# Gates of half the token groups made for all experts at once, the rest with joined high and low sums, and top-k paced

## Chip, cores and metric

The kernel runs on one core of one Trainium2 chip. The metric is the device time of one execution in microseconds (us), lower is better. A profile of one execution shows the core's engines: TensorE (PE; PEld is its weight load), VectorE (DVE), ScalarE (ACT), GpSimd (POOL) and SyncE (SP), and the DMA queues.

## What is computed

A first block (a gated recurrent mixer, then a PEER expert layer) and two attention blocks with feed-forward layers behind it, for 256 tokens of width 1024. The change is in the PEER layer alone:

```python
q = (t @ w_q).reshape(n_tok, PEER_HEADS, 2, PEER_HALF)          # 8 heads, two halves of 128
sc = jnp.einsum("thpk,hpnk->thpn", q, sub_keys)                 # 128 keys per half
s_top, i_top = lax.top_k(sc, PEER_TOPK)                         # 16 of 128, per token, head, half
cand = s_top[:, :, 0, :, None] + s_top[:, :, 1, None, :]
cand_idx = i_top[:, :, 0, :, None] * PEER_NKEYS + i_top[:, :, 1, None, :]
best, pos = lax.top_k(cand.reshape(n_tok, PEER_HEADS, 256), PEER_TOPK)
idx = jnp.take_along_axis(cand_idx.reshape(n_tok, PEER_HEADS, 256), pos, axis=-1)
g = jax.nn.softmax(best, axis=-1)
act = jax.nn.gelu(jnp.einsum("phkd,pd->phk", u_tab[idx], tb))   # 16384 experts of width 1024
out = jnp.einsum("phk,phkd->pd", g * act, v_tab[idx])
```

## The kernel before

The kernel gathers nothing. It computes the gelu products of all 16384 experts with all tokens and multiplies them by a gate that is zero where a token didn't choose an expert. The experts are 128 rows (the first index, `i`) of 128 (the second index, on the partitions).

- **q stage** (16 blocks): `weight(("q", c))`, 24 matmuls, the scores of the block before (`scores`), and x2t, the scaled input of the u stage.
- **u stage** (128 blocks, `u_block`): block i loads a 512 KB weight tile of expert row i, multiplies it with the tokens (24 matmuls of 256 columns, in three products of high and low parts: lines 209 to 211), and ScalarE writes the gelu to H, 256 columns for each row i. H lies in three pieces: rows 0 to 31, 32 to 63, 64 to 127.
- **v stage** (128 blocks): the pair of H rows is split to ph and pl (`gated`), and 12 matmuls of 512 columns (`add_k`, line 237) add it into four accumulators.

Each f32 weight tile `raw` is split into whi (ScalarE, line 188) and wlo (DVE, line 189), three tiles ahead of its use; the PE's second product of a block needs wlo.

Beside this main work runs a background generator, which `pump(n)` steps on after each block. Where a step's instructions come to stand on their engines is decided by a scheduler when the kernel is built, from what they depend on. The generators are:

- `topk()`, 90 steps at 1.6 per u block (PK) from block 0 on in the program, though the scheduler lets its first searches start in the q stage: 32 steps of the search among 128 keys (`topk1`: MAX8, FIND_INDEX8, MATCH_REPLACE8, MAX8, FIND_INDEX8 on the DVE), and then per half of the tokens the sums of candidates, the second search, the lookup of indices (products on POOL, TENSOR_REDUCE on the DVE), softmax and three transposes. It yields i1T, i2T (the two indices of each chosen expert) and gT (gate, high and low part in f16).
- `gates(0)` beside u blocks 64 to 127 and `gates(1)` beside v blocks 0 to 63. Both go over the tokens in 32 groups of 8 (TB). For a group, the DVE builds eb (one-hot of the second index, 128 x 1024 f16), ea (one-hot of the first index, 64 rows of it) and ahl (ea times gT, high and low), the PE sums them with 16 matmuls of 64 columns (line 838, 8 tokens, high and low), and the DVE multiplies the sums into H (line 844): rows 0 to 63 in `gates(0)`, rows 64 to 127 in `gates(1)`.

```python
for t in range(TB):
    g, j = t // TI, t % TI
    for q in range(2):
        pe.matmul(gps[:, t, :], eb[:, g, :, j], ahl[:, g, :, q, j], start=q == 0, stop=q == 1)
```

The gate sums and the u products share four rotating PSUM banks (`bank`); the v accumulators have four of their own.

Of the kernel before, what the change touches and what calls it, by code (L numbers as in the profile page):

```python
# [29 lines left out]
TB = 8  # L30
# [3 lines left out]
PK = 1.6  # L34
PG = 1.6
# [24 lines left out]
def kernel(  # L60
# [588 lines left out]
    with pctx:  # L649
# [54 lines left out]
        def topk():  # L704
            for tt in range(2):
                for c in range(16):
                    topk1(tt, c, c % 2)
                    yield
# [14 lines left out]
            for tt in range(2):  # L723
# [26 lines left out]
                for hh in range(8):  # L750
# [36 lines left out]

        for c in range(17):
# [22 lines left out]
        background(topk())  # L811
        Hs, H23 = [], []
# [7 lines left out]
        def gates(s):  # L820
            for t0 in range(0, T, TB):
                eb = gp.tile([128, TG, 128, TI], F16, tag="eb", name=f"eb{s}_{t0}", bufs=2)
                dve.tensor_tensor(eb, spread(i2T, t0, 128), iE.unsqueeze(1).to_broadcast([128, TG, 128, TI]),
                                  op=OP.is_equal)
                ea = gp.tile([128, TG, 64, TI], F16, tag="ea", name=f"ea{s}_{t0}", bufs=1)
                dve.tensor_tensor(ea, spread(i1T, t0, 64),
                                  iE[:, s * 64:s * 64 + 64, :].unsqueeze(1).to_broadcast([128, TG, 64, TI]),
                                  op=OP.is_equal)
                yield
                ahl = gp.tile([128, TG, 64, 2, TI], F16, tag="ahl", name=f"ahl{s}_{t0}")  # L830
                dve.tensor_tensor(ahl, ea.unsqueeze(3).to_broadcast([128, TG, 64, 2, TI]),
                                  gT[:, t0 // TI:t0 // TI + TG].unsqueeze(2).to_broadcast([128, TG, 64, 2, TI]),
                                  op=OP.mult)
                gps = bank([128, TB, 64], f"g{s}_{t0}")
                for t in range(TB):
                    g, j = t // TI, t % TI
                    for q in range(2):
                        pe.matmul(gps[:, t, :], eb[:, g, :, j], ahl[:, g, :, q, j], start=q == 0, stop=q == 1)  # L838
                yield
                for h0, n in ((0, 32), (32, 32)) if s == 0 else ((0, 64),):  # L840
                    hv = Hs[2 * s + h0 // 32][:, 0:n * T] if s == 0 else H23[0]
                    hv = hv.rearrange("p (i t) -> p i t", t=T)[:, :, t0:t0 + TB]
                    gv = gps[:, :, h0:h0 + n].rearrange("p t i -> p i t")
# [643 lines left out]
```

## Time and profile before

| | us |
|---|---|
| median of 3 runs (lowest to highest) | 1728.07 (1724.71 to 1732.78) |
| the profiled execution | 1727.79 |
| its span, first to last instruction | 1726.0 |
| PE, DVE, ACT busy in it | 1680.5, 1207.7, 884.9 |
| u stage, first to last product | 266.7 to 674.1 |
| v stage, first to last product | 674.2 to 1061.5 |

A recorded matmul is longer than the distance to the next one, since matmuls are pipelined; so costs on the PE are read from the starts of neighbours, not from the recorded durations.

### The profile page before, as it was taken

Reading aid. Unit: us, or ns where it says so; the run is one execution under the profiler, and the core shown is the slowest. Engines: PE = TensorE matmul, PEld = TensorE weight load, DVE = VectorE, ACT = ScalarE, POOL = GpSimd, SP = SyncE. Lnnn points to the kernel's source line nnn. Section 1 sums busy time; section 2 is a strip of 40 time slices with the busy share of each in tenths; the row PEclk is TensorE's granted clock in tenths of the full one; section 3 lists DMA queues with packets and bytes.
Section 4 is the critical chain, followed back from the end, with each engine's and each line's share of the span. In section 5 each row is a group of like instructions: output and inputs, shape, how many; then the busy total and the mean of one; then the engine's idle time right before and its main releaser. Section 6 shows DMA issues by size and latency. Waiting matters only on the chain.

```text
span 1726.0 us, 30134 instructions
## 1 busy us (share of the span) xinstructions
PE 1680.5 (97%) x11917; PEld 1535.0 (89%) x11917; DVE 1207.7 (70%) x2174; ACT 884.9 (51%) x1446; POOL 127.4 (7%) x104
## 2 busy tenths in 40 slices
PE   8999999999999999999999999989999999999997
PEld 8998899899999999887888888877999889989997
DVE  7969699985477776878755555876766665567665
ACT  6686565454443344344444443665655455545552
POOL 2023010430000000000000001341000000000000
PEclk9999999999999999999999999999999999999999
DMA  7645546455544445456565555632755544347551
GB/s 243 194 161 165 201 147 221 151 182 181 182 154 153 157 152 170 159 159 195 171 219 187 191 192 183 224 112 78 239 191 188 184 154 141 116 138 222 184 184 49
DMA packets 90574, 296.63 MB, mean 172 GB/s; under 512 B 9201, under 2 KB 20545, under 8 KB 89665
## 3 DMA queue, kind: packets, MB, share of 16 engines
q1 hardware_dynamic: 89088, 293.66, 52.1%
q8 instruction: 93, 1.52, 0.4%
q10 hardware_dynamic: 1344, 1.05, 0.2%
q14 instruction: 49, 0.39, 0.1%
HBM read 289.39 MB, written 3.19 MB: 170 GB/s over the span
## 4 chain that ended last, share of the span: by engine, by line
PE 81%; DVE 8%; ACT 5%; DMA 3%; issue 2%; POOL 1%; POOLq 0%; SPq 0%; ACTq 0%; DVEq 0%
PE pv L237 21%; PE ff L237 6%; PE u L209 6%; PE u L210 6%; PE u L211 6%; PE g L838 4%; DVE wlo L189 3%; PE fg L209 2%; PE fg L211 2%; PE fg L210 2%; PE fu L209 2%; PE fu L211 2%; PE fu L210 2%; PE ul L1034 1%; PE wo L237 1%
## 5 line engine op out<-in xcount | busy, mean ns | idle before, releaser
L189 DVE TENSOR_TENSOR wlo<-raw,whi 128x1024 fp32r<-128x1024 f32 x383 | 471.9, 1233 | 207.8 <-ACT whi L188 204.1
L188 ACT ACTIVATE whi<-raw 128x1024 fp32r<-128x1024 f32 x383 | 404.7, 1057 | 257.3 <-PE pv L237 122.4
L189 DVE TENSOR_TENSOR W<-raw,W 128x1024 fp32r<-128x1024 f32 x150 | 186.0, 1243 | 119.9 <-ACT W L188 119.3
L210 PE MATMUL u<-xn2h,wlo 128*128 128x256 f32 x928 | 262.5, 283 | 5.9 <-DVE wlo L189 5.8
L209 PE MATMUL u<-xn2h,whi 128*128 128x256 f32 x928 | 264.1, 285 | 0.0
L211 PE MATMUL u<-xn2l,whi 128*128 128x256 f32 x928 | 261.5, 282 | 0.0
L188 ACT ACTIVATE W<-raw 128x1024 fp32r<-128x1024 f32 x150 | 158.6, 1061 | 167.0 <-PE pv L237 68.5
L210 PEld LDWEIGHTS u<-xn2h,wlo 128*128 128x128 f32 x928 | 175.0, 189 | 8.4 <-DVE wlo L189 8.3
L209 PEld LDWEIGHTS u<-xn2h,whi 128*128 128x128 f32 x928 | 175.4, 189 | 0.0
L211 PEld LDWEIGHTS u<-xn2l,whi 128*128 128x128 f32 x928 | 174.7, 188 | 0.0
L863 ACT ACTIVATE H<-u 128x256 f32<-128x256 f32 x128 | 49.1, 384 | 220.3 <-PE u L211 220.1
L237 PE MATMUL pv<-W,ph 128*128 128x512 f32 x416 | 116.2, 391 | 0.0
L237 PE MATMUL pv<-whi,pl 128*128 128x512 f32 x304 | 96.1, 395 | 0.0
L237 PE MATMUL pv<-wlo,ph 128*128 128x512 f32 x304 | 95.5, 394 | 0.0
L237 PE MATMUL pv<-whi,ph 128*128 128x512 f32 x304 | 95.1, 402 | 0.0
L844 DVE SCALAR_TENSOR_TENSOR H<-g,H 128x256 f32<-128x256 f32 (+1 forms) x96 | 46.2, 509 | 68.3 <-PE g L838 68.3
L237 PEld LDWEIGHTS pv<-W,ph 128*128 128x128 f32 x416 | 77.7, 188 | 16.2
L838 PE MATMUL g<-ahl,eb 128*128 128x64 f16 x1024 | 73.1, 238 | 0.0
L838 PEld LDWEIGHTS <-eb 128*128 128x128 f16 x1024 | 60.3, 114 | 12.2 <-issue 9.3
L237 PEld LDWEIGHTS pv<-wlo,ph 128*128 128x128 f32 x304 | 57.1, 188 | 13.5
L237 PEld LDWEIGHTS pv<-whi,pl 128*128 128x128 f32 x304 | 57.0, 189 | 13.3
L237 PEld LDWEIGHTS pv<-whi,ph 128*128 128x128 f32 x304 | 55.7, 190 | 10.9
(843 smaller groups left out, 4244.0 us busy)
## 6 DMA issues: line engine op xcount, KB each, us to landing
raw<-in_uT_dram SPq DMA_DIRECT2D x128, 512.0 KB, 3.7
raw<-in_v_dram SPq DMA_DIRECT2D x128, 512.0 KB, 4.2
raw<-in_ff_in_dram SPq DMA_DIRECT2D x80, 512.0 KB, 3.8
raw<-in_w_in_dram SPq DMA_DIRECT2D x56, 512.0 KB, 3.9
raw<-in_ff_out_dram SPq DMA_DIRECT2D x44, 512.0 KB, 4.2
raw<-in_w_q_dram SPq DMA_DIRECT2D x16, 512.0 KB, 3.6
raw<-in_qkw_dram SPq DMA_DIRECT2D x16, 512.0 KB, 4.3
raw<-in_f_qk_dram SPq DMA_DIRECT2D x16, 512.0 KB, 4.1
```

What stands on the lines that cost most here:

```text
L188: st["hi"] = act.activation(hi, r, AF.Copy).ins
L189: st["lo"] = dve.tensor_tensor(lo, r, hi.bitcast(F32), op=OP.subtract).ins
L209: pe.matmul(o, w[0], x[0], start=start, stop=False, skip_group_check=True)
L210: pe.matmul(o, w[1], x[0], start=False, stop=False, skip_group_check=True)
L211: pe.matmul(o, w[0], x[1], start=False, stop=stop, skip_group_check=True)
L237: i = pe.matmul(acc[2 * tt + nh], x_[:, ts], w_[:, nh * 512:nh * 512 + 512], start=f, stop=l, skip_group_check=True)
L838: pe.matmul(gps[:, t, :], eb[:, g, :, j], ahl[:, g, :, q, j], start=q == 0, stop=q == 1)
L844: dve.scalar_tensor_tensor(hv, gv, 1.0 / GS, hv, op0=OP.mult, op1=OP.mult)
L863: act.activation(Hs[i // 32][:, o:o + T], ps, AF.Gelu_apprx_tanh)
L1034: done = pe.matmul(u, x_[:, k, ts], w_[:, ns], start=f, stop=l, skip_group_check=True).ins
```

## The change

Groups 0 to 15 (GM = 16) get their gates for all 128 rows at once, in the u stage. Rows whose products exist by then are multiplied by the DVE; for the others ScalarE writes the gate itself to H, and `u_block` multiplies the gelu into it later. Groups 16 to 31 get rows 0 to 63 in the u stage as before, and rows 64 to 127 in `gates_rest` beside the v blocks: one matmul of 128 columns per token there makes the high and the low sums side by side, ScalarE copies one, the DVE adds the other. The gate sums of the u stage get PSUM tiles of their own, in the banks of the accumulators (`Four.hold`). top-k starts in the q stage with one step per block, goes on at 1.35 per u block, each step is queued behind the last weight split (`paced`), and the two halves of the tokens take turns. The split rows ph and pl move to four slots in the buffers of xn2h and xn2l (`ring`).

```diff
-PK = 1.6
-PG = 1.6
+PK = 1.35
+GM = 16
...
+    class Four:
+        def hold(self, bufs=1):
+            if self.stack:
+                self.stack.close()
+            self.stack, self.n = ExitStack(), self.n + 1
+            self.pool = self.stack.enter_context(tc.tile_pool(name=f"pacc{self.n}", bufs=bufs, space=PSUM))
...
         def topk():
-            for tt in range(2):
-                for c in range(16):
-                    topk1(tt, c, c % 2)
+            for c in range(16):
+                for tt in range(2):
+                    topk1(tt, c, tt)
                     yield
...
+        def pump_behind(n):
+            with paced():
+                pump(n)
+
+        background(topk())
         for c in range(17):
...
-                t = gp.tile([128, T], F32, tag="ahl", name=f"x2t{k}")
+                t = gp.tile([128, T], F32, tag="ut", name=f"x2t{k}")
...
+            if c >= 2:
+                pump_behind(1)
...
+        def gate_apply(gps, t0, a, b):
+            m = min(max(ub["u"], a), b)
+            for hv, r, n in H_rows(a, m):
+                hv = hv[:, :, t0:t0 + TB]
+                dve.scalar_tensor_tensor(hv, gps[:, :, r - a:r - a + n].rearrange("p t i -> p i t"), 1.0 / GS, hv,
+                                         op0=OP.mult, op1=OP.mult)
+            for hv, r, n in H_rows(m, b):
+                act.activation(hv[:, :, t0:t0 + TB], gps[:, :, r - a:r - a + n].rearrange("p t i -> p i t"), AF.Copy,
+                               scale=1.0 / GS)
+
+        def gates():
+            pend = None
+            for k in range(T // TB):
+                t0, n = k * TB, 128 if k < GM else 64
+                eb, ea = one_hot(t0, 0, n)
                 yield
+                ahl = with_gates(t0, 0, n, ea)
                 yield
+                if k < GM:
+                    yield
+                gps = pacc.tile([128, TB, n], F32, tag="g", name=f"g{t0}")
+                gate_sums(gps, eb, ahl)
+                if pend:
+                    gate_apply(*pend)
+                    ub["groups"] += 1
+                pend = (gps, t0, 0, n)
                 yield
...
+        def gates_rest():
+            for t0 in range(GM * TB, T, TB):
+                eb, ea = one_hot(t0, 64, 64)
+                yield
+                ahl = with_gates(t0, 64, 64, ea)
+                yield
+                gs = gp.tile([128, 64, TB], F32, tag="gs", name=f"gs{t0}", bufs=1)
+                for h in range(2):
+                    gps = bank([128, 4, 64, 2], f"h{t0}{h}")
+                    for t in range(4):
+                        g, j = (4 * h + t) // TI, t % TI
+                        pe.matmul(gps[:, t], eb[:, g, :, j], ahl[:, g, :, :, j], start=True, stop=True)
+                    gv = gps.rearrange("p t i q -> p q i t")
+                    act.activation(gs[:, :, 4 * h:4 * h + 4], gv[:, 1], AF.Copy)
+                    yield
+                    dve.tensor_tensor(gs[:, :, 4 * h:4 * h + 4], gv[:, 0], gs[:, :, 4 * h:4 * h + 4], op=OP.add)
+                hv = H_at(64, 64)[:, :, t0:t0 + TB]
+                dve.scalar_tensor_tensor(hv, gs, 1.0 / GS, hv, op0=OP.mult, op1=OP.mult)
+                yield
...
+            n = TB * (ub["groups"] if i < 64 else min(ub["groups"], GM))
+            if n:
+                t = gp.tile([128, T], F32, tag="ut", name=f"ut{i}")
+                act.activation(t[:, 0:n], ps[:, 0:n], AF.Gelu_apprx_tanh)
+                dve.tensor_tensor(h[:, 0:n], t[:, 0:n], h[:, 0:n], op=OP.mult)
+            if n < T:
+                act.activation(h[:, n:], ps[:, n:], AF.Gelu_apprx_tanh)
...
+        pace = PK
+        for i in range(128):
             u_block(i)
-            pump(PK)
+            pump_behind(pace)
+            if bgs["gen"] is None and pace == PK:
+                pacc.hold(2)
+                background(gates())
+                pace = (3 * T // TB + GM + 1) / (125 - i)
         pump(1000)
-        background(gates(0))
-        for i in range(64, 128):
-            u_block(i)
-            pump(PG)
-        pump(1000)
-        background(gates(1))
+        pacc.hold()
+        background(gates_rest())
         acc = new_acc("pv")
+        ring = [xp.tile([128, 4, 2, T], F32R, name=f"ring{x}", tag="x" + x) for x in "hl"]
...
             add_k(acc, W, p, i == 0, False)
-            pump(PG)
+            pump(5 * (T // TB - GM) / 56)
```

The DVE's queue in the u stage, at top-k. Before, between the wlo of u block 16 and that of block 17 (`s` is the tile in which top-k works):

```order
L189 TENSOR_TENSOR wlo_3841<-raw_3723,whi_3840 128x1024
L773 RECIPROCAL s_2638<-s_2638 128x8
L743 MAX s_2638<-s_2638 128x8
L744 MAX_INDEX s_2638<-s_2638 128x8
L745 MATCH_REPLACE s_2638<-s_2638 128x50
L744 MAX_INDEX s_2638<-s_2638 128x8
L745 MATCH_REPLACE s_2638<-s_2638 128x50
L743 MAX s_2638<-s_2638 128x8 x5
L756 TENSOR_REDUCE s_2638<-s_2638 128x16
L752 TENSOR_TENSOR s_2638<-s_2638 128x800
L774 SCALAR_TENSOR_TENSOR s_2638<-s_2638 128x128
L189 TENSOR_TENSOR wlo_3883<-raw_3765,whi_3882 128x1024
```

After the change, the fullest gaps that top-k makes between two wlo in the first u blocks look like this one:

```order
L207 TENSOR_TENSOR wlo_3660<-raw_3547,whi_3659 128x1024
L716 MAX s_2634<-s_2634 128x8 x2
L717 MAX_INDEX s_2634<-s_2634 128x8
L718 MATCH_REPLACE s_2634<-s_2634 128x128
L717 MAX_INDEX s_2634<-s_2634 128x8
L718 MATCH_REPLACE s_2634<-s_2634 128x128
L719 MAX s_2634<-s_2634 128x8
L207 TENSOR_TENSOR wlo_3702<-raw_3589,whi_3701 128x1024
```

Parts of several steps, a reduction and a lookup stood between two splits; now one step or two of the same kind do, and the last instructions of top-k stand before the wlo of block 64.

The DVE's queue in the second half of the u stage, at the gates. Before:

```order
L189 TENSOR_TENSOR wlo_6502<-raw_6380,whi_6501 128x1024
L844 SCALAR_TENSOR_TENSOR H_3281<-g_72_6535,H_3281 128x32x8
L844 SCALAR_TENSOR_TENSOR H_4538<-g_72_6535,H_4538 128x32x8
L823 TENSOR_TENSOR eb_88_6675<-i2T,iE 128x1024
L831 TENSOR_TENSOR ahl_88_6679<-ea_88_6677,gT 128x1024
L189 TENSOR_TENSOR wlo_6555<-raw_6416,whi_6554 128x1024
L826 TENSOR_TENSOR ea_96_6766<-i1T,iE 128x512
```

After the change, at the same token groups:

```order
L207 TENSOR_TENSOR wlo_6504<-raw_6373,whi_6503 128x1024
L893 SCALAR_TENSOR_TENSOR H_3383<-g_6441,H_3383 128x32x8
L893 SCALAR_TENSOR_TENSOR H_4576<-g_6441,H_4576 128x32x8
L954 TENSOR_TENSOR H_5753<-ut_6534,H_5753 128x56
L893 SCALAR_TENSOR_TENSOR H_5753<-g_6441,H_5753 128x18x8
L207 TENSOR_TENSOR wlo_6560<-raw_6410,whi_6559 128x1024
L868 TENSOR_TENSOR eb_72_6594<-i2T,iE 128x1024
L871 TENSOR_TENSOR ea_72_6596<-i1T,iE 128x1024
L954 TENSOR_TENSOR H_5753<-ut_6590,H_5753 128x64
L877 TENSOR_TENSOR ahl_72_6598<-ea_72_6596,gT 128x2048
L207 TENSOR_TENSOR wlo_6601<-raw_6470,whi_6600 128x1024
```

ea and ahl are twice as wide, a third update of H (of 18 rows here) and a multiply per u block (L954) have come in.

The PE's queue in the v stage. Before, one gate set between v products (the LDWEIGHTS and MATMUL pair stands 16 times in a row):

```order
L237 MATMUL pv_8546<-wlo_9495,ph_9532 128x512
L237 MATMUL pv_8547<-wlo_9495,ph_9532 128x512
L838 LDWEIGHTS eb_128_9554
L838 MATMUL g_128_9578<-ahl_128_9576,eb_128_9554 128x64
L237 MATMUL pv_8544<-whi_9536,ph_9596 128x512
```

After, the matmuls of one token group (each pair stands four times in a row):

```order
L255 MATMUL pv_8768<-whi_8796,ringl 128x512
L255 MATMUL pv_8769<-whi_8796,ringl 128x512
L933 LDWEIGHTS eb_144_8968
L933 MATMUL h_9013<-ahl_144_8992,eb_144_8968 128x128
L933 MATMUL h_9020<-ahl_144_8992,eb_144_8968 128x128
L255 MATMUL pv_8766<-wlo_8797,ringh 128x512
```

32 sets of 16 matmuls have become 32 runs of four (two for each of 16 groups), which the scheduler places side by side or apart. In the u stage there are 32 sets of 16 before and after, in blocks 64 to 126.

## Rows read from the trace of the kernel before

**Rows 1.** The page: busy us of an engine, share of the span, instructions.
```profile
PE 1680.5 (97%) x11917; PEld 1535.0 (89%) x11917; DVE 1207.7 (70%) x2174; ACT 884.9 (51%) x1446; POOL 127.4 (7%) x104
```

**Rows 2.** Instructions on tile u: durations min/median/max in ns, first and last start.
```profile
L209 PE MATMUL u<-xn2h,whi x928: 274/281/368, 300.7 to 673.9; 128*128 128x256 f32 x186
...
L209 PE MATMUL u<-s,whi x96: 281/281/365, 266.7 to 300.4; 128*128 128x256 f32 x96
```

**Rows 3.** PE timeline, u stage, one gate set: start us, duration us, instruction.
```profile
502.52 1.12 PE L838 MATMUL g<-ahl,eb 128*128 128x64 f16 x16
503.45 0.36 PE L209 MATMUL u<-xn2h,whi 128*128 128x256 f32 x1
503.66 0.28 PE L210 MATMUL u<-xn2h,wlo 128*128 128x256 f32 x1
```

**Rows 4.** PE timeline, v stage, one gate set.
```profile
866.45 1.12 PE L838 MATMUL g<-ahl,eb 128*128 128x64 f16 x16
867.37 0.71 PE L237 MATMUL pv<-whi,ph 128*128 128x512 f32 x2
867.92 0.62 PE L237 MATMUL pv<-whi,pl 128*128 128x512 f32 x2
868.38 0.62 PE L237 MATMUL pv<-wlo,ph 128*128 128x512 f32 x2
```

**Rows 5.** The chain that ended last, q stage: start us, us, what.
```profile
219.74 0.44 PE sc L688 x4
```

**Rows 6.** Waits of the PE, 200 to 1070 us: total, times, longest.
```profile
PE u L210 <- DVE wlo L189: 5.8, 8, 1.6
```

**Rows 7.** Stretches of the u stage: length, busy us of each engine, clock, DMA.
```profile
266.70:300.40 33.70, 33.70 (x289) 33.70 (x288) 33.40 (x165) 17.54 (x28) 0.00 (x0) 1.00 0.71 239
300.60:380.00 79.40, 73.51 (x593) 71.00 (x592) 75.28 (x190) 40.51 (x56) 35.93 (x16) 1.00 0.51 163
380.00:463.00 83.00, 83.00 (x697) 83.00 (x697) 40.28 (x42) 38.76 (x64) 0.00 (x0) 1.00 0.56 184
463.00:674.00 211.00, 211.00 (x2018) 209.70 (x2018) 148.55 (x225) 84.59 (x127) 0.00 (x0) 1.00 0.48 158
```

**Rows 8.** PE timeline, second attention: bf16 matmuls of 128 columns.
```profile
1436.33 0.22 PE L1180 MATMUL s<-maskb,identb 128*128 128x128 bf16 x1
1436.38 0.22 PE L1371 MATMUL s<-C,sel 128*128 128x128 bf16 x1
1436.44 0.22 PE L1180 MATMUL s<-maskb,identb 128*128 128x128 bf16 x1
1436.50 0.65 PE L1176 MATMUL s<-kz,fqq 128*128 128x256 f32 x2
```

**Rows 9.** Groups of instructions, 300 to 1100 us: busy us, mean ns.
```profile
L831 DVE TENSOR_TENSOR ahl<-ea,gT 128x1024 f16<-128x1024 f16 x64 | 43.7, 683 | 0.0
...
L823 DVE TENSOR_TENSOR eb<-i2T,iE 128x1024 f16<-128x1024 f16 x64 | 43.5, 680 | 0.0
L319 ACT ACTIVATE ph<-H 128x512 fp32r<-128x512 f32 x64 | 39.3, 616 | 2.3 <-PE pv L237 2.3
...
L826 DVE TENSOR_TENSOR ea<-i1T,iE 128x512 f16<-128x512 f16 x64 | 26.7, 417 | 0.0
```

**Rows 10.** Instructions on tile g: durations min/median/max in ns.
```profile
L844 DVE SCALAR_TENSOR_TENSOR H<-g,H x96: 411/424/693, 466.3 to 874.2; 128x256 f32<-128x256 f32 x64, 128x512 f32<-128x512 f32 x32
```

**Rows 11.** Groups of instructions on the DVE, 200 to 267 us: busy us, mean ns.
```profile
L189 DVE TENSOR_TENSOR wlo<-raw,whi 128x1024 fp32r<-128x1024 f32 x18 | 22.0, 1221 | 6.2 <-ACT whi L188 6.1
L699 DVE FIND_INDEX8 s<-s 128x8 uint32<-128x128 f32 x28 | 7.9, 284 | 0.0
L698 DVE MAX8 s<-s 128x8 f32<-128x128 f32 x28 | 6.8, 279 | 0.0
...
L700 DVE MATCH_REPLACE8 s<-s 128x128 f32<-128x128 f32 x14 | 3.8, 275 | 0.0
...
L699 DVE MATCH_VALUE_LOAD s<-s 128x8 f32 x28 | 2.2, 77 | 0.0
```

More of the change, by code (lines that the diff above doesn't have):

```diff
@@ L351 @@
     sks = []
-    for tag, n, b in (("eb", 4, 2), ("ph", 2, 2), ("pl", 2, 2)):
-        for j in range(2):
+    for tag, n, b in (("eb", 4, 2), ("ea", 4, 1), ("gs", 4, 1)):
+        for j in range(b):
             t = gp.tile([128, n, 128], F32, tag=tag, name=f"sk{tag}{j}", bufs=b)
@@ L775, in topk @@
                                          zs.unsqueeze(2).to_broadcast([128, 8, 16]), op0=OP.mult, op1=OP.mult)
+                for _ in range(3):
+                    yield
                 tp = bank([128, 3, 128], f"tk{tt}")
@@ L810, with H_part, H_rows, H_at @@
         nc.sync.dma_start(xn2l.bitcast(F32), x2l.bitcast(F32))
-        background(topk())
-        Hs, H23 = [], []
+        Hs = []
+        HR = (0, 32, 64, 128)
+        ub = {"u": 0, "groups": 0}
+        def H_part(k):
+            while len(Hs) <= k:
+                n = (HR[len(Hs) + 1] - HR[len(Hs)]) * T
+                Hs.append((xp.tile([128, n], F32, name="H0", tag="H0"),) if not Hs else
+                          (hp.tile([128, n], F32, tag=("", "H1", "H23")[len(Hs)], name=f"H{len(Hs)}"),))
+            return Hs[k][0]
+        def H_rows(a, b):
+            for k in range(3):
+                lo, hi = max(a, HR[k]), min(b, HR[k + 1])
+                if lo < hi:
+                    yield H_part(k)[:, (lo - HR[k]) * T:(hi - HR[k]) * T].rearrange("p (i t) -> p i t", t=T), lo, hi - lo
+        def H_at(i, n=1):
+            return next(H_rows(i, i + n))[0]
         TG = TB // TI
@@ L818, in spread @@
             return row[:, t0:t0 + TB].rearrange("p (g j) -> p g j", j=TI).unsqueeze(2).to_broadcast([128, TG, n, TI])
[L820 to L828, printed above, removed]
-                yield
[L830 to L838, printed above, removed]
-                yield
[L840 to L843, printed above, removed]
-                    dve.scalar_tensor_tensor(hv, gv, 1.0 / GS, hv, op0=OP.mult, op1=OP.mult)
@@ new lines, in one_hot @@
+        def one_hot(t0, a, n):
+            eb = gp.tile([128, TG, 128, TI], F16, tag="eb", name=f"eb{a}_{t0}", bufs=2)
+            dve.tensor_tensor(eb, spread(i2T, t0, 128), iE.unsqueeze(1).to_broadcast([128, TG, 128, TI]),
+                              op=OP.is_equal)
+            ea = gp.tile([128, TG, n, TI], F16, tag="ea", name=f"ea{a}_{t0}", bufs=1)
+            dve.tensor_tensor(ea, spread(i1T, t0, n),
+                              iE[:, a:a + n, :].unsqueeze(1).to_broadcast([128, TG, n, TI]), op=OP.is_equal)
+            return eb, ea
@@ new lines, in with_gates, with gate_sums @@
+        def with_gates(t0, a, n, ea):
+            ahl = gp.tile([128, TG, n, 2, TI], F16, tag="ahl", name=f"ahl{a}_{t0}")
+            dve.tensor_tensor(ahl, ea.unsqueeze(3).to_broadcast([128, TG, n, 2, TI]),
+                              gT[:, t0 // TI:t0 // TI + TG].unsqueeze(2).to_broadcast([128, TG, n, 2, TI]),
+                              op=OP.mult)
+            return ahl
+        def gate_sums(gps, eb, ahl):
+            for t in range(TB):
+                g, j = t // TI, t % TI
+                for q in range(2):
+                    pe.matmul(gps[:, t, :], eb[:, g, :, j], ahl[:, g, :, q, j], start=q == 0, stop=q == 1)
```

39 lines of the change are left out of this document (21 added, 18 removed).

## Prediction

> **What bounds the kernel now.** I read the page's busy shares first: TensorE (PE) is busy 97% of the span [rows 1], so the time is the PE's work plus the few places where it waits. Next the list of the u products, for the pace without gates: block 0 starts at 266.7 us and block 12 at 300.7, so a block of 24 matmuls takes 34.0 / 12 = 2.83 us [rows 2]. Then the timeline around one gate set. Its 16 matmuls start at 502.52, the next u matmul at 503.45, and the one behind that 0.21 us later where 2.83 / 24 = 0.118 is usual: 0.93 + 0.09 = 1.02 us of the PE for a set, 57 ns for each matmul with its weight load [rows 3]. In the v stage the same set costs 0.92 + (0.55 - 0.46) = 1.01 us [rows 4]. There are 64 sets, so the gates cost some 65 us of the PE, half in u blocks 64 to 127 and half in v blocks 0 to 63.
>
> The same list gives what is lost in the u stage. From block 12 at 300.7 to the last L209 start at 673.9, with the 0.35 us of that matmul and the two behind it, are 373.5 us. The products need 116 x 2.83 = 328.3 and 32 gate sets 32.6 [rows 2, 3]; 12.6 us are left. Some 0.7 are the six transposes of top-k, if one costs what an f32 score matmul of 128 columns does (0.44 for four [rows 5]); about 12 us are stalls. The table of waits names them: L210 of u waits for wlo from VectorE (DVE), 5.8 us in 8 waits [rows 6]. That is less than 12 because a recorded matmul lasts 0.28 us where the next starts after 0.12, which hides the head of each wait, and a matmul that follows a wait restarts late as after a gate set. The stretches say where: the DVE is busy 33.40 of 33.70 us in u blocks 0 to 11 and 75.28 of 79.40 in the next 28, and the PE only 73.51 of those 79.40; from 380 on the DVE has 40.28 of 83.00 and the PE never waits [rows 7]. So top-k is crammed into the end of the q stage, where the scheduler put 14 of its 32 first searches [rows 11], and the first 40 u blocks, makes wlo late there, and leaves the DVE half idle behind.
>
> **The change, part by part.** *Gates in the v stage.* Before, 32 token groups each issue 16 matmuls of 64 columns here. Now only groups 16 to 31 do, with high and low columns in one matmul: two runs of four matmuls of 128 columns. Removed are 32 x 1.01 = 32.3 us. The price of a 128-column matmul with its own load isn't in this place of the trace. The nearest rows are the bf16 ones of the second attention: 128-column matmuls, each with its weight load, start at 1436.33, 1436.38, 1436.44, and the next matmul at 1436.50, so 0.17 / 3 = 57 ns, what 64 columns cost [rows 8]. With 57 ns as the lower bound, the upper bound from near rows adds 64 columns at the u matmul's rate (0.118 us / 256 = 0.46 ns each), 87 ns; further off, 118 ns, as for 256 columns, if steps in the f16 operand cost double. I take 57, since those rows have the type size, the columns and the load in common. A run of four is 0.23 + 0.09 for the return to the 512-column matmuls = 0.32, and 32 runs are 10.2. **Term 1: -32.3 + 10.2 = -22.1 us.**
>
> The Trainium skill ("TensorE: Matmul & The Clock Gate", Back-to-back issue gap) speaks against this: a stream of load and matmul pairs with 128 columns runs at about 81 ns per matmul. Here 384 matmuls of 128 columns are issued (256 in the u stage, 128 in the v stage), so by the page the sum would come out 384 x 0.024 = 9 us worse; the row of 57 ns disagrees with it, on three intervals only.
>
> *Gates in the u stage.* Groups 0 to 15 now take all 128 rows at once: 16 matmuls of 128 columns instead of 64, at the same 57 ns. Groups 16 to 31 are as before. So 32 sets of 16 remain: **term 2: 0** (upper bound 256 x 0.030 = +7.7). They lie in the same u blocks 64 to 126. The DVE pays instead. Its busy time in this stretch is 148.55 of 211.00 us [rows 7]. Added: ea of 1024 instead of 512 elements, 16 x (0.680 - 0.417) = 4.2; ahl of 2048 instead of 1024, at most 16 x 0.683 = 10.9; a third scalar_tensor_tensor for rows from 64 up to the block reached, at most 16 x 0.424 = 6.8; and one multiply per u block, 64 x 0.3 = 19, taken between nothing and the 0.424 of 256 elements, since its width grows from 8 to 128 columns [rows 9, 10]. That makes 190 of 213 us, 89%, still below the 95% at which the stalls above came. ScalarE gets a second gelu piece per block and 16 copies of gates; it is busy 84.59 of 211.00 [rows 7] and could double that. Both are covered by the PE; if the cover fails, the PE waits in the gate set for ahl or in L210 for wlo.
>
> *Top-k.* The same work is spread: 1 step per q block, 1.35 per u block, each queued behind the weight split, so it ends at block 62 and not near 40. A step of the 128-key search is two MAX8, two FIND_INDEX8, one MATCH_REPLACE8 and three loads of values: 2 x 0.279 + 2 x 0.284 + 0.275 + 3 x 0.077 = 1.63 us at most, and 1.40 where the loads hide [rows 11]. By the order, 13 of the 32 steps stand in the q stage and 19 in the first 15 u blocks: with 1.22 for wlo the DVE has 1.22 + 19/15 x (1.40 to 1.63) = 2.99 to 3.28 per block of 2.83 [rows 2, 11]. The excess over the 15 blocks is 2.4 to 6.8 us in all, and the three weight buffers run about two blocks (5.7 us) ahead, so some 0 to 1 reaches the PE. After that the load falls. As a check: the DVE's work in blocks 0 to 63 was 33.40 + 75.28 + 40.28 = 149 us [rows 7], of 64 x 2.83 = 181. In a q block one step, wlo and half of x2t's multiply and split (256 elements each, as an H update 0.42) make at most 1.63 + 1.22 + 0.42 = 3.27, and the PE has 2.83 + 0.44 with the scores [rows 5, 10, 11]: no gain, perhaps 1 us lost. **Term 3: -12 + 2 = -10 us** (bounds 0 and -12).
>
> *From u to v.* The split rows (ring) now live in the buffers of xn2h and xn2l, so the first split, 0.616 us on ScalarE [rows 9], can only start when the last u matmul is over. The PE has the first eight joined matmuls (0.6) meanwhile. The accumulators take the banks of the last gate set, which is read earlier: 35 u matmuls, 4 us, stand behind that set in the order. **Term 4: +1** (0 to 3).
>
> Sum: -22.1 + 0 - 10 + 1 = -31 us. The profiled execution took 1727.8 us (span 1726.0 and 1.8 around it), which is the median of the runs, 1728.07, within their spread; 1727.8 - 31 = **1697 us**.
>
> **The rivals.** *128 columns are dear.* The extra columns are not hidden behind the weight load: 87 ns instead of 57 for 384 matmuls gives back 11.3 us, 1708; at 118 ns 23 us, 1720. For it: the f16 operand is read in steps of two and four elements, which the rows of 57 ns may not have. Against it: [rows 8]. The page named above would put it at 1706.
>
> *The DVE stall moves.* The gate phase at 89% is as lumpy as top-k was at 95%; it loses the same 12 us in its 64 blocks: 1709. For it: some blocks carry ea, eb, two or three H updates and wlo, about 4 us, against 2.83 or, with a set, 3.85 of the PE. Against it: a neighbour block is lighter each time, and the H updates wait for nothing.
>
> *Slower.* One mechanism: eb, ea and ahl of one group are a chain on the DVE behind the split, ea has a single buffer, and the set stands in the middle of a u block, so the PE waits at each of the 32 sets for ahl. It gives back the gain at 31 / 32 = 1 us per set, and is slower by over 0.5% from (31 + 8.6) / 32 = 1.2 us on. Against it: the set is issued one step behind ahl for the wide groups, and the 211 us of before hold no such wait: PE busy 211.00 [rows 7].
>
> *The change does little.* Dear columns at 118 ns and a moved stall together: 1697 + 23 + 12 = 1732, no difference.
>
> **How the numbers follow.** A change of 0.5%, 8.6 us, is about what can be told from none. Forecast 0.62, dear columns 0.15, moved stall 0.13, little 0.05, slower 0.05. The first, and the next two except at their far ends, are faster by over 0.5%: 0.88. Same 0.08 (little, and the far ends), slower 0.04. The range goes from 1689 (all of top-k's stalls gone, no cost at the turn, and five us of slack in the small prices) to 1712, which takes in both middle rivals at their near prices.
>
> **What would show it.** Joined matmuls in the v stage in runs of four, 0.23 us apart from run start to the next 512-column matmul; wide sets in the u stage of 0.92 us as before. If they show 1.4 or more, term 1 and 2 are wrong. The u products from block 0 to 63 without waits for wlo, some 182 us; else term 3 is wrong. The DVE at some 190 us in the stretch of blocks 64 to 127, with that stretch still near 213; if it is longer at an unchanged set price, the stall has moved. The first v product about 1 us behind the last u. The v stage should shrink by 22 us, and the last u product start about 10 us earlier than at 673.9.

## Result and profile after

The changed kernel takes 1707.03 us (median of 4 runs, 1705.95 to 1709.14), the kernel before 1727.86 (4 runs, 1724.71 to 1732.78): a ratio of 0.9878, 95% interval 0.9853 to 0.9904. It is faster by 20.8 us. The prediction was 1697, with a range of 1689 to 1712: 10 us too much gain. The profiled execution of after took 1709.1 us (span 1707.4), the highest of its four, so between the two traces 18.6 us of span have gone.

Busy shares of after, beside [rows 1], and the u products by tile, beside [rows 2] (durations min/median/max in ns, first and last start):

```profile
PE 1666.7 (98%) x11533; PEld 1525.5 (89%) x11533; DVE 1229.4 (72%) x2220; ACT 902.1 (53%) x1556; POOL 121.6 (7%) x104
```
```profile
L229 PE MATMUL u<-xn2l,whi x928: 277/284/373, 297.9 to 676.7; 128*128 128x256 f32 x186
L227 PE MATMUL u<-s,whi x96: 276/276/369, 264.9 to 297.3; 128*128 128x256 f32 x96
```

The waits of the PE from 200 to 1070 us, beside [rows 6]:

```profile
PE q L227 <- ACT hgh L660: 1.7, 2, 1.5
PE tp L650 <- DVE hk L645: 0.2, 1, 0.2
```

The eight waits for wlo are gone, and none for ahl has come. The stretches of the u stage, beside [rows 7] (length, then busy us of PE, PEld, DVE, ACT, POOL, then clock, DMA):

```profile
264.90:297.60 32.70, 32.70 (x291) 32.70 (x290) 30.80 (x128) 17.55 (x28) 0.00 (x0) 1.00 0.72 242
297.80:380.00 82.20, 82.20 (x695) 82.20 (x694) 75.28 (x201) 42.09 (x64) 14.13 (x8) 1.00 0.61 189
380.00:447.00 67.00, 67.00 (x562) 67.00 (x561) 59.15 (x102) 34.01 (x52) 14.14 (x8) 1.00 0.58 184
447.00:677.30 230.30, 230.30 (x2059) 228.61 (x2057) 177.66 (x305) 95.78 (x206) 0.00 (x0) 1.00 0.47 147
```

Block 64 begins at 447.2 us instead of 459.4, without a wait. But the 64 blocks behind it, with the gate sets, take 229.5 us (first to last product) where they took 214.7, although the PE waits for nothing. The first product of block 64 in the kernel before:

```profile
459.39 0.28 PE L209 MATMUL u<-xn2h,whi 128*128 128x256 f32 x1
```

The timeline of the PE after shows why the blocks are longer. Its three pieces are a wide set (16 matmuls of 128 columns, groups 0 to 15), a set of 64 columns (groups 16 to 31), and the turn from u to v:

```profile
447.99 2.03 PE L886 MATMUL g<-ahl,eb 128*128 128x128 f16 x16
449.76 0.37 PE L228 MATMUL u<-xn2h,wlo 128*128 128x256 f32 x1
...
600.52 1.12 PE L886 MATMUL g<-ahl,eb 128*128 128x64 f16 x16
601.46 0.36 PE L227 MATMUL u<-xn2h,whi 128*128 128x256 f32 x1
...
676.67 0.28 PE L229 MATMUL u<-xn2l,whi 128*128 128x256 f32 x1
676.79 0.65 PE L933 MATMUL h<-ahl,eb 128*128 128x128 f16 x8
677.55 1.20 PE L255 MATMUL pv<-whi,ringh 128*128 128x512 f32 x4
678.59 0.65 PE L933 MATMUL h<-ahl,eb 128*128 128x128 f16 x8
679.05 0.71 PE L255 MATMUL pv<-whi,ringl 128*128 128x512 f32 x2
```

From the start of the wide set to the next product are 1.77 us, 111 ns for each matmul, and not the 0.92 that was forecast. The set of 64 columns in the second piece takes 0.94, as in [rows 3]. The third piece is the turn from u to v: eight joined matmuls, also of 128 columns, take 679.05 - 678.59 = 0.46 us, 57 ns each, as forecast. So not all matmuls of 128 columns are dear, only those of the u stage. The two differ in how the columns lie in ahl. The step, here and below, is the distance in elements between neighbouring columns of the operand that streams past the loaded weights. For one token and one part (q) the row index moves in steps of four f16 elements (8 bytes), since high, low and two tokens (TI) stand innermost; the joined matmul reads high and low too, and its columns are two elements (4 bytes) apart. They also differ in that the wide ones add in pairs into the same PSUM columns.

### The profile page after: what moved, and what is told of

Same layout as the page of the kernel before. It is cut to its first block, busy times and chain, and to the rows that moved or that the text cites. A ratio compares the mean times of both kernels' runs of the same rounds, so it can differ in the third digit from the quotient of the medians.

```text
span 1707.4 us, 29521 instructions
## 1 busy us (share of the span) xinstructions
PE 1666.7 (98%) x11533; PEld 1525.5 (89%) x11533; DVE 1229.4 (72%) x2220; ACT 902.1 (53%) x1556; POOL 121.6 (7%) x104
## 4 chain that ended last, share of the span: by engine, by line
PE 87%; DVE 5%; ACT 4%; DMA 2%; issue 2%; POOL 1%; POOLq 0%; SPq 0%; ACTq 0%; DVEq 0%
PE pv L255 21%; PE u L229 7%; PE u L227 7%; PE u L228 7%; PE ff L255 6%; PE g L886 3%; PE fg L229 2%; PE fg L227 2%; PE fg L228 2%; PE fu L227 2%; PE fu L229 2%; PE fu L228 2%; DVE wlo L207 1%; PE dpv L255 1%; PE ul L1132 1%
## 5 line engine op out<-in xcount | busy, mean ns | idle before, releaser
L227 PE MATMUL u<-xn2h,whi 128*128 128x256 f32 x928 | 263.4, 284 | 0.0
L227 PEld LDWEIGHTS u<-xn2h,whi 128*128 128x128 f32 x928 | 175.3, 189 | 0.0
L255 PE MATMUL pv<-W,ringh 128*128 128x512 f32 x384 | 106.3, 391 | 0.0
L255 PE MATMUL pv<-whi,ringh 128*128 128x512 f32 x288 | 91.8, 399 | 0.1
L255 PE MATMUL pv<-whi,ringl 128*128 128x512 f32 x288 | 91.7, 395 | 0.0
L255 PE MATMUL pv<-wlo,ringh 128*128 128x512 f32 x288 | 89.8, 395 | 0.0
L255 PEld LDWEIGHTS pv<-W,ringh 128*128 128x128 f32 x384 | 71.6, 188 | 14.9
L255 PEld LDWEIGHTS pv<-whi,ringl 128*128 128x128 f32 x288 | 54.1, 188 | 12.8
L255 PEld LDWEIGHTS pv<-wlo,ringh 128*128 128x128 f32 x288 | 53.9, 188 | 12.6
L255 PEld LDWEIGHTS pv<-whi,ringh 128*128 128x128 f32 x288 | 53.1, 188 | 11.8 <-ACT ringh L337 0.3
L255 PE MATMUL ff<-W,fph 128*128 128x512 f32 x192 | 59.3, 398 | 1.1 <-ACT fph L337 1.1
L255 PE MATMUL pv<-W,ringl 128*128 128x512 f32 x192 | 59.3, 390 | 0.0
```

The lines of the kernel that those rows point to most:

```text
L227: pe.matmul(o, w[0], x[0], start=start, stop=False, skip_group_check=True)
L255: i = pe.matmul(acc[2 * tt + nh], x_[:, ts], w_[:, nh * 512:nh * 512 + 512], start=f, stop=l, skip_group_check=True)
```

## Experiments

The ratios below are to runs of the kernel before taken beside them on the same chip; x5 to x8 ran on one chip, the others on another. The intervals of x1, x5, x6, x8 and x9 overlap or touch, so the 2 to 4 us between their medians are not clear of noise; for these the stages of the traces decide.

**x1, step two.** The high and the low part stand outside the rows, so all gate matmuls read at a step of two.

```diff
-            ahl = gp.tile([128, TG, n, 2, TI], F16, tag="ahl", name=f"ahl{a}_{t0}")
-            dve.tensor_tensor(ahl, ea.unsqueeze(3).to_broadcast([128, TG, n, 2, TI]),
-                              gT[:, t0 // TI:t0 // TI + TG].unsqueeze(2).to_broadcast([128, TG, n, 2, TI]),
+            ahl = gp.tile([128, TG, 2, n, TI], F16, tag="ahl", name=f"ahl{a}_{t0}")
+            dve.tensor_tensor(ahl, ea.unsqueeze(2).to_broadcast([128, TG, 2, n, TI]),
+                              gT[:, t0 // TI:t0 // TI + TG].unsqueeze(3).to_broadcast([128, TG, 2, n, TI]),
...
-                    pe.matmul(gps[:, t, :], eb[:, g, :, j], ahl[:, g, :, q, j], start=q == 0, stop=q == 1)
+                    pe.matmul(gps[:, t, :], eb[:, g, :, j], ahl[:, g, q, :, j], start=q == 0, stop=q == 1)
...
```

> Only the layout of ahl differs from the changed kernel: high and low stand outside the rows, so the 128 columns that a gate matmul reads stand two f16 elements (4 bytes) apart and not four (8 bytes). The wide sets took 1.77 us to the next u matmul, 111 ns per matmul, where the joined matmuls of the v stage, two elements apart, took 57 ns. Theory 1, the step of four elements is what costs: the wide sets fall to about 0.93 us, the stretch of u blocks 64 to 127 from 230.3 to about 217 us, and the time to 1707 - 16 x 0.84 = 1693.6; if the sets of 64 columns were held by the same step they fall below 0.93 as well, by up to half (another -7). Theory 2, the pair of matmuls that adds into the same PSUM columns is what costs when it is 128 wide (the joined matmuls of the v stage don't add): the sets stay at 1.77 and the time at 1707. A multiply that is slower on VectorE in this layout would show in ahl's duration (1.22 us for 2048 elements) and, if the cover fails, as waits of TensorE.

Measured: 1686.23 us (5 runs, 1685.12 to 1686.87), ratio 0.9763 (0.9749 to 0.9776). A wide and a narrow set in its timeline, the stretch of blocks 64 to 127, and the u products:

```profile
447.80 1.13 PE L886 MATMUL g<-ahl,eb 128*128 128x128 f16 x16
448.74 0.37 PE L228 MATMUL u<-xn2h,wlo 128*128 128x256 f32 x1
...
595.10 0.65 PE L886 MATMUL g<-ahl,eb 128*128 128x64 f16 x16
595.59 0.36 PE L229 MATMUL u<-xn2l,whi 128*128 128x256 f32 x1
```
```profile
447.00:655.30 208.30, 208.30 (x2058) 206.80 (x2056) 175.73 (x304) 95.75 (x206) 0.00 (x0) 1.00 0.50 163
```
```profile
L227 PE MATMUL u<-xn2h,whi x928: 274/282/368, 297.5 to 654.5; 128*128 128x256 f32 x186
L227 PE MATMUL u<-s,whi x96: 276/276/369, 264.7 to 297.1; 128*128 128x256 f32 x96
```

The wide set falls from 1.77 to 0.94 us, though it still adds in pairs: the adding is out. The narrow set falls too, from 0.94 to 0.49. So the 57 ns of a 64-column matmul, which the prediction read from [rows 3, 4], was itself the price of the step. 16 x 0.83 + 16 x 0.45 = 20.5 us, and the time fell by 20.8. VectorE's multiply costs the same in this layout: 1219 ns on average for the wide groups, where it was 1220.

**x2, all groups joined in the v stage.** The changed kernel with one number different.

```diff
-GM = 16
+GM = 0
```

> GM is 0 instead of 16: no group gets its gates for all rows at once, all 32 have 64 rows in the u stage and 64 rows as joined sums in the v stage. By the prices read in the changed kernel (wide set 1.86 with its surroundings, narrow set 1.02, joined run of four 0.32) the u stage loses 16 x 0.84 = 13.4 us, and a few more where the updates of H and the second gelu piece go, and the v stage gains 32 runs x 0.32 = 10.2: 1707 - 13 + 10 = 1704, down to 1700. Theory of the prediction (wide sets cost what narrow ones cost): the u stage would stay and the time would be 1707 + 10 = 1717. Rival: VectorE and ScalarE don't keep up with twice the joined groups in v blocks 0 to 63, and TensorE waits there: over 1710.

Measured: 1708.38 us (4 runs, 1705.34 to 1709.21), ratio 0.9888 (0.9873 to 0.9903). Its u products and a wait of the PE:

```profile
L229 PE MATMUL u<-xn2l,whi x928: 278/282/365, 296.8 to 660.8; 128*128 128x256 f32 x186
```
```profile
PE pv L255 <- ACT ringh L337: 3.6, 1, 3.6
```

This is above the 1704 that was worked out. The u stage ends 15.9 us earlier than in the changed kernel, 1.1 of it because it starts earlier; the rest is near the 13.4 that the dear wide sets say. The v products run from 661.7 to 1039.2, 14.1 longer than the 677.6 to 1041.0 of after: the 10 us of 32 more runs, and one wait of 4 us at the turn for the split of the first rows. So it isn't 1717, as equal prices would have it, and the 4 us above 1704 are about that wait, which I had put only in the rival.

**x3, prices.** Between the u and the v stage stand runs of 16 matmuls with their loads, which nothing reads, of n columns at a step of s elements:

```diff
...
+        for nm, n, st_, acc_ in (("mA", 64, 4, 0), ("mB", 128, 4, 0), ("mC", 128, 4, 1), ("mD", 128, 2, 0),
+                                 ("mE", 128, 1, 0), ("mF", 64, 2, 0), ("mG", 64, 1, 0), ("mH", 128, 8, 0),
+                                 ("mI", 256, 2, 0), ("mJ", 256, 4, 0), ("mK", 256, 1, 0)):
+            mp = bank([128, 512], nm)
+            for r in range(16):
+                c = (r // 2 if acc_ else r) % (512 // n) * n
+                pe.matmul(mp[:, c:c + n], me[:, r // 2 % 4, :, r % 2], mf[:, r % 2:r % 2 + (n - 1) * st_ + 1:st_],
+                          start=not acc_ or r % 2 == 0, stop=not acc_ or r % 2 == 1)
...
```

Behind them come seven runs (nA to nG) of 24 matmuls as in a u block, with the moving operand (the columns that stream) at offsets of 0, 64, 128, 576, 1600, 32 and 1024 bytes in xn2h and xn2l.

> Added between the u and the v stage, with results that nothing reads: runs of 16 f16 matmuls, each with its own weight load, with 64, 128 and 256 moving columns at steps of 1, 2, 4 and 8 elements, one of them with pairs that add into the same PSUM columns; and seven runs of 24 u-like matmuls whose moving operand starts at different offsets. The time itself means nothing (some 40 us are added); the distances of the starts do. Theory 1 (step): 128 columns cost 57 ns at steps 1 and 2 and about 111 at step 4, with and without adding; 256 columns 107 to 118 at step 2 and about 220 at step 4; 64 columns at step 4 57 and at step 2 no more. Theory 2 (adding): at step 4 only the adding run costs 111. For the u-like runs: the changed kernel's u products took 0.113 us each on x2h and 0.119 on xn2h; if the place of the operand decides, some offset shows 0.113, if not all stay at 0.119.

The timeline of the PE (the difference of two starts, divided by 16, is the price of one matmul with its load):

```profile
676.09 1.12 PE L978 MATMUL mA<-ahl,eb 128*128 128x64 f16 x16
677.03 2.05 PE L978 MATMUL mB<-ahl,eb 128*128 128x128 f16 x16
678.90 2.05 PE L978 MATMUL mC<-ahl,eb 128*128 128x128 f16 x16
680.77 1.14 PE L978 MATMUL mD<-ahl,eb 128*128 128x128 f16 x16
681.74 1.06 PE L978 MATMUL mE<-ahl,eb 128*128 128x128 f16 x16
682.64 0.66 PE L978 MATMUL mF<-ahl,eb 128*128 128x64 f16 x16
683.13 0.64 PE L978 MATMUL mG<-ahl,eb 128*128 128x64 f16 x16
683.61 3.79 PE L978 MATMUL mH<-ahl,eb 128*128 128x128 f16 x16
687.22 2.02 PE L978 MATMUL mI<-ahl,eb 128*128 128x256 f16 x16
689.08 3.79 PE L978 MATMUL mJ<-ahl,eb 128*128 128x256 f16 x16
692.69 1.93 PE L978 MATMUL mK<-ahl,eb 128*128 128x256 f16 x16
694.38 0.37 PE L227 MATMUL nA<-xn2h,whi 128*128 128x256 f32 x1
```

| ns per matmul | step 1 | step 2 | step 4 | step 8 |
|---|---|---|---|---|
| 64 columns | 30 | 31 | 59 | |
| 128 columns | 56 | 61 | 117 (adding in pairs: 117) | 226 |
| 256 columns | 106 | 116 | 226 | |

The price goes with the columns, from 64 on, and with the step from two elements on: twice at four, four times at eight. The weight load sets no floor above 30 ns here, and adding costs nothing. The Trainium skill ("TensorE: Matmul & The Clock Gate", Back-to-back issue gap) has 81 ns for a load and matmul pair of 128 columns; the run has 56 to 61 at steps one and two and 117 at step four, so no single figure holds here. The Trainium skill ("SBUF — State Buffer", Specifications (TRN2)) also puts full bandwidth at two or more hits in each line of 16 bytes. A step of four f16 elements makes two and cost twice as much, so the measurement speaks against that rule for this operand.

Of the u-like runs, the one at offset 0 keeps 0.1185 us per matmul (2.37 us for 20 intervals), and that at 64 bytes 0.1135 (1.93 for 17):

```profile
694.82 0.28 PE L227 MATMUL nA<-xn2h,whi 128*128 128x256 f32 x1
...
697.19 0.28 PE L229 MATMUL nA<-xn2l,whi 128*128 128x256 f32 x1
...
698.02 0.28 PE L227 MATMUL nB<-xn2h,whi 128*128 128x256 f32 x1
...
699.95 0.28 PE L229 MATMUL nB<-xn2l,whi 128*128 128x256 f32 x1
...
705.66 0.28 PE L227 MATMUL nE<-xn2h,whi 128*128 128x256 f32 x1
...
708.27 0.28 PE L229 MATMUL nE<-xn2l,whi 128*128 128x256 f32 x1
```

The other five fall in line, each read in the same way: 0.1135 at 576 and at 1600 bytes (nD, nE), 0.119 at 128 and at 1024 bytes (nC, nG), 0.117 at 32 (nF). While nB to nG ran, the other engines and the DMA were all but idle; there the pace follows the place of the operand, counted modulo 128 bytes.

**x4, top-k as it was**, with the changed gates:

```diff
-PK = 1.35
+PK = 1.6
...
-            for c in range(16):
-                for tt in range(2):
-                    topk1(tt, c, tt)
+            for tt in range(2):
+                for c in range(16):
+                    topk1(tt, c, c % 2)
                     yield
...
-                for _ in range(3):
-                    yield
...
-        background(topk())
...
-            if c >= 2:
-                pump_behind(1)
...
+        background(topk())
         Hs = []
...
-            pump_behind(pace)
+            (pump if pace == PK else pump_behind)(pace)
```

> The changed kernel with top-k as it was: 32 first searches and the rest started behind the q stage in the program, the halves of the tokens one after the other, 1.6 steps per block, not queued behind the weight split. The gates stay as changed. Theory (top-k's crowding made wlo late, 12.6 us): TensorE waits for wlo again between u blocks 12 and 40, and the time is 1707 + 10 to 13 = 1717 to 1720. Rival: the gates' way of waiting in the queue or the earlier end of the q stage gave the 13 us, and the time stays within 3 us of 1707. Also: if crowding on VectorE set the pace of u blocks 0 to 11, their matmuls go from 0.113 back to 0.118 us.

Measured: 1717.66 us (4 runs, 1715.27 to 1718.96), ratio 0.9940 (0.9925 to 0.9955); 10.6 us longer than the changed kernel. Its waits of the PE, 200 to 1070 us, the stretch of blocks 12 to 40, and blocks 0 to 11:

```profile
PE u L228 <- DVE wlo L207: 5.9, 8, 1.5
```
```profile
299.20:380.00 80.80, 74.74 (x604) 72.24 (x603) 76.35 (x190) 40.56 (x57) 35.93 (x16) 1.00 0.51 163
```
```profile
L227 PE MATMUL u<-s,whi x96: 281/281/367, 265.1 to 298.7; 128*128 128x256 f32 x96
```

The eight waits are back, and so is the loss. The u stage from its first to its last product takes 422.3 us (265.1 to 687.4) where the changed kernel has 411.8 (264.9 to 676.7). Blocks 0 to 11 also fall back, from 32.8 us to 34.0, so 1.2 of the loss are pace and some 9 are the waits. Whether the crowding of VectorE set that pace is not shown: in x8 these blocks take 34.0 us with top-k spread as in the changed kernel.

**x5 and x6, the place of the moving operands.** x5 puts xn2h, xn2l and the rings 64 bytes further on, from x1:

```diff
-        xn2h = xp.tile([128, KC, T], F32R, name="xn2h", tag="xh")
-        xn2l = xp.tile([128, KC, T], F32R, name="xn2l", tag="xl")
+        def shifted(name, tag):
+            return xp.tile([128, KC * T + 32], F32R, name=name, tag=tag)[:, 16:KC * T + 16]
+
+        xn2h, xn2l = [shifted("xn2" + x, "x" + x).rearrange("p (a b) -> p a b", a=KC) for x in "hl"]
...
-        ring = [xp.tile([128, 4, 2, T], F32R, name=f"ring{x}", tag="x" + x) for x in "hl"]
+        ring = [shifted(f"ring{x}", "x" + x).rearrange("p (s a b) -> p s a b", s=4, a=2) for x in "hl"]
```

> The kernel of x1 (1686.2 us), with the operands that the u products (xn2h, xn2l) and the v products (the rings) read as moving data placed 64 bytes further on, so that they begin at 64 and not at 0 modulo 128 bytes. Theory (the place of the moving operand sets the pace): the u products of blocks 12 to 127 go from 0.1188 to 0.1133 us each, 24 x 116 x 0.0055 = 15 us, and the v products gain up to as much per matmul, 1536 x 0.0055 = 8: 1671, down to 1663. Rival (the place does not decide alone, since the u products on x2h of the kernel before and of x4 lay at 64 modulo 128 too and took 0.118): 1686.

x6 moves x2h and x2l instead, from x1:

```diff
-        x2h = s2[:, 0:2048].rearrange("p (a b) -> p a b", a=8)
-        x2l = s2[:, 2048:4096].rearrange("p (a b) -> p a b", a=8)
+        x2h = s2[:, 16:2064].rearrange("p (a b) -> p a b", a=8)
+        x2l = s2[:, 2064:4112].rearrange("p (a b) -> p a b", a=8)
```

> The kernel of x1, with x2h and x2l, the moving operands of u blocks 0 to 11, placed 64 bytes further on, at 0 modulo 128 bytes. Theory (place): these 288 products go from 0.1133 back to 0.1188 us, 1.6 us, and the time from 1686.2 to 1687.8. Rival: the pace of these blocks comes from what VectorE does beside them (top-k crowded or not), and stays at 0.113: 1686.2.

Measured: x5 1682.21 us (5 runs, 1679.39 to 1685.08), ratio 0.9744 (0.9728 to 0.9760); x6 1687.13 (4 runs, 1686.29 to 1687.40), ratio 0.9769 (0.9753 to 0.9784). The u products of x5, then of x6:

```profile
L227 PE MATMUL u<-xn2h,whi x928: 275/280/370, 295.9 to 649.6; 128*128 128x256 f32 x186
```
```profile
L227 PE MATMUL u<-xn2h,whi x928: 274/281/367, 298.2 to 654.5; 128*128 128x256 f32 x186
L227 PE MATMUL u<-s,whi x96: 283/283/365, 263.5 to 297.8; 128*128 128x256 f32 x96
```

In x6 blocks 0 to 11 take 298.2 - 263.5 = 34.7 us, 1.9 more than the 32.8 of x1, as the theory of the place says. In x5 the first L227 of block 12 and the last of block 127 are 353.7 us apart, against 356.3 in x6 and 357.0 in x1, which have xn2h unmoved: 2.6 to 3.3 us, not the 15 that the theory asked for. The v products, whose rings were moved too, gained nothing: first to last they take 365.4 us in x5 (650.7 to 1016.1) and 363.5 in x1 (655.6 to 1019.1). And x4 and x8 had 34.0 us in blocks 0 to 11 with x2h unmoved. So the place has a part in the pace, but does not decide it beside the work of the other engines.

**x7, the kernel before with step two** (the same edit of ahl as in x1, nothing else).

> The kernel before, with nothing changed but the layout of ahl: high and low outside the rows, so that its gate matmuls of 64 columns read elements two apart and not four. Theory (columns times step set the price, as in the price runs: 64 columns 58 ns at step 4 and 30 at step 2): all 64 gate sets fall from 0.93 to 0.49 us, and the time by 64 x 0.44 = 28 us, from 1727.2 to 1699, more than the change itself gave (21). Rival (the sets were held by their weight loads or by the waits around them): 1727.

Measured: 1702.52 us (4 runs, 1700.10 to 1705.06), ratio 0.9860 (0.9841 to 0.9879). A gate set in its timeline, and its wait:

```profile
499.81 0.66 PE L838 MATMUL g<-ahl,eb 128*128 128x64 f16 x16
500.30 0.37 PE L209 MATMUL u<-xn2h,whi 128*128 128x256 f32 x1
```
```profile
PE u L210 <- DVE wlo L189: 6.2, 8, 1.8
```

The set falls from 0.93 [rows 3] to 0.49 us. 24.9 of the 28 us arrive. The v products, first to last, shrink by 13.6 us, from 387.3 to 373.7 (661.8 to 1035.5), near the 14 of their 32 sets. From block 12 to the last L209 the u stage shrinks by 11.5, from 373.2 [rows 2] to 361.7 (299.7 to 661.4): most of what is missing lies there, and what takes it was not found. One layout of one tile, without any of the change, gives at least what the change did (the intervals of the two ratios overlap), while top-k's waits stay as they were.

**x8, all groups wide**, from x1:

```diff
-GM = 16
+GM = 32
```

> The kernel of x1 with GM 32: all groups get their gates for all 128 rows in the u stage, and none is left for the v stage. By the prices (wide set 0.93 + 0.09, narrow set 0.49 + 0.09, two joined runs 2 x 0.32) 16 groups save 0.2 us each: 1686.2 - 3.2 = 1683. Rival: VectorE, busy 175.7 of 208.3 us in u blocks 64 to 127 of x1, gets some 20 us more (ea, ahl and the third update of 16 more groups) in 215, 91%, and TensorE waits in the sets: over 1688.

Measured: 1683.78 us (4 runs, 1683.24 to 1685.14), ratio 0.9750 (0.9734 to 0.9765): 2.4 below x1 by the medians, where 3.2 were worked out. Blocks 64 to 127, and the u products:

```profile
447.00:661.70 214.70, 214.42 (x2048) 212.80 (x2047) 192.57 (x315) 102.01 (x223) 0.00 (x0) 1.00 0.50 158
```
```profile
L227 PE MATMUL u<-xn2h,whi x928: 274/282/368, 297.3 to 660.9; 128*128 128x256 f32 x186
L227 PE MATMUL u<-s,whi x96: 280/282/368, 263.3 to 297.0; 128*128 128x256 f32 x96
```

VectorE is busy 192.57 of 214.70 us, 90%, and the PE waits for none of its gate work. Blocks 0 to 11 take 297.3 - 263.3 = 34.0 us, 1.2 more than in x1, although the edit touches neither top-k nor x2h.

**x9, the rest not joined**, from x1: one tile of PSUM per group, the 16 matmuls of `gate_sums`, and the multiply into H straight from PSUM.

```diff
-                gs = gp.tile([128, 64, TB], F32, tag="gs", name=f"gs{t0}", bufs=1)
...
-                        pe.matmul(gps[:, t], eb[:, g, :, j], ahl[:, g, :, :, j], start=True, stop=True)
-                    gv = gps.rearrange("p t q i -> p q i t")
-                    act.activation(gs[:, :, 4 * h:4 * h + 4], gv[:, 1], AF.Copy)
-                    yield
-                    dve.tensor_tensor(gs[:, :, 4 * h:4 * h + 4], gv[:, 0], gs[:, :, 4 * h:4 * h + 4], op=OP.add)
+                gps = bank([128, TB, 64], f"h{t0}")
+                gate_sums(gps, eb, ahl)
+                yield
+                yield
...
-                dve.scalar_tensor_tensor(hv, gs, 1.0 / GS, hv, op0=OP.mult, op1=OP.mult)
+                dve.scalar_tensor_tensor(hv, gps.rearrange("p t i -> p i t"), 1.0 / GS, hv, op0=OP.mult, op1=OP.mult)
```

> The kernel of x1, with the high and low sums of the v stage (groups 16 to 31, rows 64 to 127) not joined: 16 matmuls of 64 columns at a step of two elements that add into the same PSUM columns, and VectorE multiplies them into H straight from PSUM, without the copy on ScalarE and the two additions. Theory (columns times step set the price, a matmul with its load has no other floor above 30 ns): 0.49 + 0.09 us per group where two joined runs cost 0.46 + 0.09 to 0.18: 1686.2, within 1.5 us. Rival (joining pays because it halves the number of matmuls, as the prediction had it, 16 x 57 against 8 x 57 ns): 16 x 0.46 = 7 us longer, 1693.

Measured: 1688.20 us (4 runs, 1684.37 to 1688.96), ratio 0.9775 (0.9760 to 0.9790), by the medians 2.0 above x1, a little outside what I had allowed and far from 1693. In the traces the way from the last u product to the last v product is 364.7 us (653.6 to 1018.3), 0.3 more than in x1 (654.7 to 1019.1). A set in its v stage:

```profile
775.22 0.66 PE L886 MATMUL h<-ahl,eb 128*128 128x64 f16 x16
775.71 0.71 PE L255 MATMUL pv<-W,ringh 128*128 128x512 f32 x2
```

16 matmuls of 64 columns take 0.49 us; the eight joined ones took 0.46. Joining as such buys almost nothing.

**x10, together**: x5 with GM = 32.

> All that shortened the time so far: step two, the shifted operands of x5 and GM 32 of x8. x8 stood 2.4 us below x1 and x5 4.0; if both add up, 1680. Rival: the pace of the u products is set by something other than the place and x5's gain does not return: 1684.

Measured: 1680.17 us (5 runs, 1677.98 to 1681.72), ratio 0.9725 (0.9711 to 0.9738). Its median is the lowest of all, 47.5 us below the kernel before and some 27 below the changed one. Of these 27, 20.8 are the layout of x1.

## Why the prediction was right in sign and too good by 10 us

Between the two traces, by stage: the first u product comes 1.8 us earlier, blocks 0 to 11 are 1.2 shorter and blocks 12 to 63 9.2; blocks 64 to 127 are 14.8 longer; from the last u product to the last v product 23.1 are gone; behind it 1.9 are lost, which I didn't look into (x1, with the same code there, loses 0.3). That is the -18.6.

- **Term 1, v stage (-22.1) with term 4, the turn (+1).** Forecast -21.1, measured -23.1. A joined matmul costs 57 ns as taken, runs of four go by in 0.22 us. The first v product comes 0.88 us behind the last u product's start; without the 0.12 of that product and the 0.46 of the joined matmuls, 0.3 us are lost. The size was right, the picture behind it was not: the gain did not come from half as many matmuls, each as dear as before. The joined columns stand two elements apart instead of four, and x9 and x7 show the same price per group without joining.
- **Term 2, gates of the u stage (0).** This is the step that failed: "16 matmuls of 128 columns instead of 64, at the same 57 ns". They cost 111 ns, and 16 sets x (1.77 - 0.93) = 13.4 of the 14.8 us are theirs. The other 1.4 lie for the most part in the pace of the u products between the sets. I had seen 57 ns for 64 columns at a step of four [rows 3] and 57 ns for 128 columns [rows 8], and read the equality as a floor that columns do not move. It was a coincidence of two prices, 64 columns at double cost and 128 at single cost. The far bound, 118 ns "if steps in the f16 operand cost double", was the truth for the wide sets; I had put it aside because [rows 8] shared type size, columns and load, though not the step: the mask that they read lies contiguously, at a step of one.
- **Term 3, top-k (-10).** The mechanism was right. Blocks 0 to 63 take 447.2 - 264.9 = 182.3 us, where some 182 were forecast, without a wait for wlo: 10.4 less than before. x4 brings the waits back, and 10.6 us. That the size fits is in part luck. The stalls were 9.2 us and not 12: the prediction took 2.83 us for every block, the pace of blocks 0 to 11, where blocks 12 to 63 without a stall need (447.2 - 297.7) / 52 = 2.87. The other 1.2 are the quicker pace of blocks 0 to 11, which no term had. The q stage, where 1 us of loss was feared, lost none.
- **The rivals.** "128 columns are dear" named a price of 1708, near the result, but for all 384 matmuls at 87 ns; 128 of them kept 57 and 256 went to 111. The stall did not move: VectorE had 177.66 of 230.30 us in the gate blocks, 77%, and in x8 even 90% made no wait. The PE did not wait for ahl at any set.

What stays open: what sets the pace of the u products. They take between 0.113 and 0.120 us each, steady over a whole stretch. With the other engines idle the place of the operand went with it (x3). Beside the main work it did not decide: x2h, unmoved, was read at 0.114 us in the changed kernel and at 0.118 in x4 and x8, and xn2h, moved, at 0.118 in x5. Crowding on VectorE would fit x4, but not x8.

## What to carry to other kernels

Before a matmul is made wider, look how far apart in bytes its moving columns lie: here a step of four f16 elements doubled the price and a step of eight made it four times as dear, while steps of one and two cost nearly the same. When two different instructions show the same price, that is not yet a floor; vary the width and the step by itself in one run before a term rests on it. And try the layout first: reordering one tile gave 20.8 us on top of the change and 24.9 without it, where the restructuring around it gave 20.8.

## What the runs showed of the hardware that was not expected

- A load and matmul pair of 64 f16 columns took 30 ns at steps of one and two elements, 59 at four; 128 columns 56, 61, 117 and 226 ns at steps of 1, 2, 4 and 8; 256 columns 106, 116 and 226 at 1, 2 and 4 (x3).
- Contiguous f32 columns are 4 bytes apart, like f16 columns at a step of two, and cost about the same: 256 of them 0.118 us in the u blocks, against 0.116 (x3, mI).
- A multiply of 2048 f16 elements on VectorE that writes the parts apart cost no more than one that interleaves them: 1219 against 1220 ns (x1).
- With the other engines all but idle, f32 products of 256 columns took 0.1135 us each with the moving operand 64, 576 or 1600 bytes into its tile, 0.117 at 32, and 0.1185 to 0.1195 at 0, 128 and 1024 (x3).
